# Layer 0 of a hybrid diffusion backbone: a shorter projection prologue, and the work between attention tiles pinned to a place

## The chip, the cores and the metric

The kernel runs on one core of one Trainium2 chip, in one launch. The core has five engines with instruction streams of their own: TensorE (PE, matmul), VectorE (DVE), ScalarE (ACT), GpSimd (POOL) and SyncE (SP, which here only issues DMAs). The metric is device time in microseconds (us); the kernel is timed in several runs and one more execution is profiled.

## The reference

Two layers run over 1024 latent tokens and a context prefix of 256 tokens, width 1024, all in float32. The change touches layer 0 alone. Its core, cut:

```
h_lat = rms_norm(x_lat, norm_g) * (1 + sc) + sh           # adaLN from c; h_ctx alike from c_ctx
aq, ak, av, ag, bq, bk, bv, bg = split_cols(h @ w_in, (512, 128, 128, 512, 512, 128, 128, 512))
aq, ak = rms_norm(aq, q_gain), rms_norm(ak, k_gain)       # A alone
aq, ak, bq, bk = rope(...)                                # latent tokens alone
oa = softmax(aq ka^T / 8) va                              # A: 8 heads, 2 key heads, keys = ctx + all latents
ob = softmax([bq kb^T / 8 + band, sink]) vb               # B: ctx + latents within 128, sink logit per head
y = concat([oa * silu(ag), ob * silu(bg)]) @ w_out        # also for the context tokens
x = x + g * y
```

Layer 1 (a conformer convolution and a 2-D neighbourhood attention) and a final RMSNorm follow.

## The kernel before, in words

**Precision.** Each float32 matmul is done as three matmuls of a fast format: every operand is split into a high part (a cast on ACT) and a low part (a subtraction on POOL or DVE, `split`, lines 307 to 310), and `mm3` (lines 327 to 329) adds high x high, high x low and low x high.

**Units.** Layer 0's attention is cut into four units `u`, each of four query heads that share one key head. Units 0 and 1 are A (global, with the RMSNorm of queries and keys), 2 and 3 are B (banded, with a sink). They run in the order `ORDER = (2, 3, 0, 1)`: B, B, A, A. I call them first to fourth unit, and the last one the fourth.

**Projection.** `proj_qkv(u)` computes queries, keys and values of a unit in ten blocks of 128 tokens (`j` = 0, 1 context, 2 to 9 latent), 24 matmuls of 384 columns each (PSUM name `pq`), two blocks to a step `jp`. A block is copied to SBUF (`pc`), normed (units 0 and 1: square, reduce, a reciprocal root by Newton steps, ten small multiplications, line 835), rotated (`rt`, lines 846 to 850), and then taken by `qk_tail`: three PE transposes (`trk`), splits, a store of the queries to DRAM (`Q<-qs`) and keys into the SBUF tile `KA`. `proj_gate(u, ms)` computes the SiLU gate of a unit in six pieces (`m` = two halves of the channels, `c` = three chunks of 256, 512 and 512 tokens; 24 matmuls, name `pg`) and stores it to DRAM (`G<-sg`). Both are generators that yield three times a block, which I call pieces: a piece is some 8 matmuls.

**Attention.** `attn_gen` runs over groups (a unit and a block of 128 queries, in the order `QORD`, ten to a unit), and in a group over tiles of 128 keys: two score matmuls (`st`), for a band edge a mask, exponent on ACT, `split` into `ph` and `pl`, and three more matmuls (`ov`) three tiles later (`LOOK0`). B has 42 tiles a unit, A 84. Each tile yields twice: a step. Before a group's tiles stands its preparation (`attn_prep`): it loads the queries (`QH`, `QL`), takes a bound of the scores by extra matmuls with a maximum on DVE (`mx`, `mp`), and writes it with the sink into `QL`; it is spread over the tiles of the group two ahead. A group ends with `finish`: transposes of the denominators, products (`y`), the gate (`gt`, loaded by `gate()` at the middle tile) and a store (`Od<-y`), or, in the last unit, a split in place. `KB`, a copy of the keys in another tile, is made by `load_kb` in two DMAs at a unit's first group; there is one `KB` for all units, and two `KA` and two `V`.

**What lies where.** `weave(main, n, fill, k)` takes `n` attention steps and lays `k` pieces of `fill` between them. The fill's instructions get a lower priority (`later(80)`); the compiler's list scheduler orders each engine's stream by priority and readiness as it estimates them. With `lag` > 0, each fill instruction is also held behind the score matmul `lag` scores back (`issue_after(sts[-lag])`, on PE's stream alone). Before the change layer 0 never uses it, so that fill may stand in PE's stream far ahead of its place in the program. The attention steps of layer 0 are 12 of preparation, then 84, 84, 168 and 168, and fill is laid as follows: the whole first projection and half of its gate run alone (`solo`), the other half in the first 9 steps; then the next unit's projection and half of its gate in the middle of a unit's steps, the other half of its gate at the start of the next unit; the last `NLAST` steps of a unit (28 or 48) have none. In the fourth unit lie the loads of earlier outputs (`load_oh`) and the output projection (`po`) of the first two units in 65 steps, of the third in 41, of the fourth (`final_proj`, with the residual's norm and the next layer's h, `norm_h`) in the rest, for the chunks that are complete; the last chunk comes after the attention.

**Modulation.** The pieces of the projections also tick `mods`, which computes the rest of the adaLN vectors (`pm`, from weights `mw`): every `TICK0` = 1 piece while solo, every `TICK1` = 3 afterwards.

## Time and profile before

| what | us |
|---|---|
| median of 3 runs | 1579.01 (1578.08 to 1581.34) |
| the profiled execution | 1581.59 |
| its span, first to last instruction | 1579.8 |
| PE busy in the span | 1469.3 |
| DVE, POOL, ACT busy | 1086.9, 794.1, 748.8 |

A row of the profile names the source line, the engine, the operation, out<-in by the program's tile names, and the shapes; "x" is a count. Stretches are in us from the span's start. "PEld" is the load of a matmul's stationary operand, which overlaps the matmuls. The granted clock is a share of TensorE's full clock. Layer 0 covers about the first 950 us.

### The profile page before, as it was taken

The page shows a single profiled execution, that of the slowest core. Times are in us where ns is not written, and L with a number is a line of the kernel's source. Part 1 is how long each engine was busy: PE and PEld are TensorE (multiplying, and loading weights), DVE is VectorE, ACT ScalarE, POOL GpSimd, SP SyncE. Part 2 cuts the span into 40 slices and gives each one's busy share as a digit, 9 for nine tenths or more (in the row PEclk, how much of TensorE's full clock was granted, in tenths as well). Part 3 has the DMA queues.
Part 4 walks back from the last instruction along what each step waited for, and adds up shares of the span by engine and source line. Part 5 has one row for each costly group of instructions (what it writes and reads, how often), then busy time and mean ns, then how long its engine had stood idle before and what let it go on. Part 6 is the DMA issues. An engine that isn't in the chain of part 4 may idle for free.

```text
span 1579.8 us, 21684 instructions
## 1 busy us (share of the span) xinstructions
PE 1469.3 (93%) x7084; PEld 1172.7 (74%) x7084; DVE 1086.9 (69%) x2279; ACT 748.8 (47%) x1418; POOL 794.1 (50%) x637
## 2 busy tenths in 40 slices
PE   6899999998998999999999879999989999989995
PEld 2785987886886767876766657888877878768874
DVE  2833576588589865566677856999738466787866
ACT  3722333443435555447556654433334355554563
POOL 3531352553445666557556754664532244364665
PEclk8899999998999999999999989999999999979997
DMA  9473324422312253222112022222595577967632
GB/s 367 151 238 127 114 84 153 137 76 90 110 44 82 87 195 129 64 57 62 41 30 88 7 66 77 86 68 72 175 271 194 186 215 218 284 191 231 187 110 107
DMA packets 158105, 208.23 MB, mean 132 GB/s; under 512 B 15068, under 2 KB 96168, under 8 KB 157992
## 3 DMA queue, kind: packets, MB, share of 16 engines
q1 hardware_dynamic: 151328, 195.27, 39.1%
q10 hardware_dynamic: 6664, 11.57, 2.2%
q8 instruction: 56, 0.92, 0.3%
q14 instruction: 57, 0.47, 0.1%
HBM read 152.27 MB, written 53.22 MB: 130 GB/s over the span
## 4 chain that ended last, share of the span: by engine, by line
PE 73%; DVE 15%; DMA 6%; ACT 2%; issue 2%; POOL 1%; SPq 0%; ACTq 0%; DVEq 0%; POOLq 0%
PE p L327 6%; PE p L328 6%; PE p L329 6%; PE ov L447 4%; PE ov L449 4%; PE po L327 4%; PE po L329 4%; PE po L328 4%; PE ov L448 4%; PE st L491 4%; PE st L495 4%; PE pq L327 3%; PE pq L328 3%; PE pq L329 3%; PE pg L329 2%
## 5 line engine op out<-in xcount | busy, mean ns | idle before, releaser
L310 POOL TENSOR_TENSOR pl<-pf,ph 128x512 fp32r<-128x512 f32 (+4 forms) x321 | 392.9, 1235 | 362.8 <-ACT ph L307 280.0
L503 ACT ACTIVATE pf<-st 128x512 f32<-128x512 f32 x284 | 166.0, 596 | 213.7 <-PE st L495 159.2
L310 POOL TENSOR_TENSOR wl<-wr,wh 128x512 fp32r<-128x512 f32 (+2 forms) x131 | 168.7, 1300 | 187.8 <-ACT wh L307 145.9
L307 ACT CAST ph<-pf 128x512 fp32r<-128x512 f32 (+4 forms) x364 | 210.0, 588 | 19.6 <-PE ov L448 9.5
L327 PE MATMUL p<-hh,wh 128*128 128x512 f32 x448 | 180.0, 402 | 11.7 <-ACT wh L307 6.2
L328 PE MATMUL p<-hl,wh 128*128 128x512 f32 x448 | 179.6, 402 | 1.2 <-POOL hl L310 1.2
L329 PE MATMUL p<-hh,wl 128*128 128x512 f32 x448 | 176.3, 399 | 0.0
L491 PE MATMUL st<-QH,KAt 128*128 128x512 f32 (+4 forms) x364 | 142.5, 392 | 7.6 <-DVE pf L500 4.7
L447 PE MATMUL ov<-ph,Vt 128*128 128x512 f32 (+4 forms) x364 | 141.9, 390 | 5.5 <-DVE y L652 3.4
L449 PE MATMUL ov<-pl,Vt 128*128 128x512 f32 (+4 forms) x364 | 142.5, 391 | 4.5 <-POOL pl L310 3.5
L448 PE MATMUL ov<-ph,Vt 128*64 128x512 f32 (+4 forms) x364 | 139.9, 384 | 0.0
L495 PE MATMUL st<-QL,KBt 68*128 68x512 f32 (+4 forms) x364 | 135.8, 386 | 0.0
L307 ACT CAST wh<-wr 128x512 fp32r<-128x512 f32 (+2 forms) x134 | 80.8, 612 | 98.4 <-PE p L328 21.2
L1068 DVE SCALAR_TENSOR_TENSOR cps<-U,taps,cps 128x512 f32<-128x512 f32 x184 | 126.3, 749 | 0.9
L327 PEld LDWEIGHTS p<-hh,wh 128*128 128x128 f32 x448 | 85.4, 191 | 33.0 <-ACT wh L307 7.1
L615 DVE TENSOR_REDUCE mp<-mx 128x1 f32<-128x512 f32 x128 | 85.7, 682 | 25.7 <-PE mx L614 25.2
L328 PEld LDWEIGHTS p<-hl,wh 128*128 128x128 f32 x448 | 85.5, 191 | 21.7 <-POOL hl L310 2.2
L329 PEld LDWEIGHTS p<-hh,wl 128*128 128x128 f32 x448 | 85.3, 190 | 20.6 <-issue 0.5
L449 PEld LDWEIGHTS ov<-pl,Vt 128*128 128x128 f32 x364 | 70.5, 194 | 28.9 <-POOL pl L310 9.9
L327 PE MATMUL pq<-wh,hh 128*128 128x384 f32 x256 | 88.5, 346 | 2.8 <-ACT hh L307 2.8
L491 PEld LDWEIGHTS st<-QH,KAt 128*128 128x128 f32 x364 | 70.0, 192 | 26.3 <-ACT pf L503 6.9
L329 PE MATMUL pq<-wh,hl 128*128 128x384 f32 x256 | 87.4, 341 | 0.0
(277 smaller groups left out, 3482.6 us busy)
## 6 DMA issues: line engine op xcount, KB each, us to landing
mw<-in_mod_w_dram SPq DMA_DIRECT2D x16, 1024.0 KB, 5.7
Q<-qs SPq DMA_DIRECT2D x40, 256.0 KB, 2.1
QH<-Q SPq DMA_DIRECT2D x80, 128.0 KB, 2.7
mw<-in_mod_w_dram SPq DMA_DIRECT2D x16, 512.0 KB, 6.5
wr<-in_od_d_dram SPq DMA_DIRECT2D x32, 256.0 KB, 2.9
wr<-in_ev_qkv_dram SPq DMA_DIRECT2D x16, 384.0 KB, 5.1
KAt<-KD SPq DMA_DIRECT2D x16, 384.0 KB, 5.8
wr<-in_od_wo_dram SPq DMA_DIRECT2D x22, 256.0 KB, 3.3
```

The lines of the kernel that those rows point to most:

```text
L307: acts.append(SC.copy(hi, src))
L310: (GP if leng == "g" else VE).tensor_tensor(lo, src, hi.bitcast(F32), op=ALU.subtract)
L327: PE.matmul(o, lh, rh, start=first, stop=False)
L328: PE.matmul(o, lh, rl, start=False, stop=False)
L329: PE.matmul(o, ll, rh, start=False, stop=last)
L447: PE.matmul(o, V[:, 64:192], ph[:, :n], start=(t == 0), stop=False)
L448: PE.matmul(g.ov[0:64, q0 : q0 + n], V[:, 0:64], ph[:, :n], start=False, stop=False)
L449: PE.matmul(o, V[:, 64:192], pl[:, :n], start=False, stop=(last and g.sink is None))
L491: sts.append(PE.matmul(st[:, :n], KA[:, cs], g.QH[:, q0 : q0 + n], start=True, stop=False))
L495: PE.matmul(st[:, :n], KB[0:68, cs], g.QL[0:68, q0 : q0 + n], start=False, stop=True)
L503: acts.append(SC.activation(pf[:, :n], st[:, :n], AF.Exp, scale=1.0 if g.bias else SCALE))
L1068: VE.scalar_tensor_tensor(pc, uc, w, pc, op0=ALU.mult, op1=ALU.add)
```

## The change

The constants `N0`, `NLAST`, `GB` and `NFILL` go; `LAG0 = 3` comes, `TICK1` goes from 3 to 2, `O1` from (6, 65, 41, 14) to (6, 80, 42, 22). `proj_qkv` takes a list of block pairs, so that a unit's projection can be cut in two, and ends by emptying its `tails`. `load_g0`, which brought the first unit's gate weights through the attention's `ph` and `pl` buffers, goes; those weights now use the projection's weight buffers like the others. Solo are now only the first six blocks of the first unit. Then one list says what is laid into the attention steps, with every fill pinned three scores back: the first unit's other four blocks into the 12 preparation steps, its gate for chunk 1 into 6, the rest of its gate and the second projection into 70, the second gate and the third projection into 72, the third gate, fourth projection and fourth gate into 200. The key copies are cut at 384 and 768; the banded units copy the last part only at their third group. In layer 0 `gate()` is called at a group's last tile. The output projection is pinned likewise, and has 80 and 42 steps instead of 65 and 41; the final part then has 28 steps for 22 pieces instead of 44 for 14. `ready` and the assertions on it only check the order while the program is built, and leave no instruction.

```
-            if t == len(g.tiles) // 2:
+            if t == (len(g.tiles) // 2 if layer[0] else len(g.tiles) - 1):
                 g.gate()
...
-        for ks in (slice(0, 512), slice(512, NTOK)):
+        i = QORD.index(qb)
+        parts = {0: ((0, 384), (384, 768), (768, NTOK))} if u < 2 else {0: ((0, 384), (384, 768)), 2: ((768, NTOK),)}
+        for k0, k1 in parts.get(i, ()):
+            ks = slice(k0, k1)
             SY.dma_start(KBs[u][0:64, ks].bitcast(F32), KAs[u][0:64, ks].bitcast(F32))
...
-                gw[u] = load_g0(u) if u == ORDER[0] else load_w0("ev_g", u)
+                gw[u] = load_w0("ev_g", u)
...
-        def proj_qkv(u, w):
-            wh, wl = w or load_w0("ev_qkv", u)
-            new_kv(u)
-            for jp in range(5):
+        def proj_qkv(u, jps, w=None):
+            if jps[0] == 0:
+                gw[u, 0] = w or load_w0("ev_qkv", u)
+                new_kv(u)
+            wh, wl = gw[u, 0]
+            for jp in jps:
...
+            while tails:
+                qk_tail(*tails.pop(0))
...
-        for _ in fill0(0, w0):
+        def gates(u, *cs):
+            return proj_gate(u, [(m, c) for c in cs for m in range(2)])
+
+        for _ in proj_qkv(ORDER[0], (0, 1, 2), w0):
             pass
...
-        for k in range(4):
-            u = ORDER[k]
-            n = NSTEP[u // 2] + (12 if k == 0 else 0)
-            if k < 3:
-                n0 = N0[1 + u // 2] if k else N0[0]
-                n1 = n - n0 - NLAST[u // 2]
-                weave(main, n0, proj_gate(u, gblocks(k)[1]), 9, False)
-                weave(main, n1, fill0(k + 1), NFILL[k], False)
-                weave(main, NLAST[u // 2], iter(()), 0, False)
-            else:
-                weave(main, GL, proj_gate(u, gblocks(k)[1]), 18 - 3 * GB, False)
+        A, B, C, D = ORDER
+        full = range(5)
+        for n, fill, k in ((12, [proj_qkv(A, (3, 4))], 12),
+                           (6, [gates(A, 1)], 6),
+                           (70, [gates(A, 0, 2), proj_qkv(B, full)], 42),
+                           (72, [gates(B, 1, 0, 2), proj_qkv(C, full)], 48),
+                           (188 + GL, [gates(C, 1, 0, 2), proj_qkv(D, full), gates(D, 1, 0, 2)], 66)):
+            weave(main, n, chain(*fill), k, False, True, LAG0)
...
-        weave(main, O1[1], out0_part(parts[0]), 48, False)
-        weave(main, O1[2], chain(load_oh(parts[1]), out0_part(parts[1])), 30, False)
+        weave(main, O1[1], out0_part(parts[0]), 48, False, True, LAG0)
+        weave(main, O1[2], chain(load_oh(parts[1]), out0_part(parts[1])), 30, False, True, LAG0)
```

More of the change, by code (lines that the diff above doesn't have):

```diff
@@ L66 @@
 LATE = 100
-GB = 2
-NFILL = (39, 39, 36)
 GL = 12
 HV = 'gggvvvvg'
-O1 = (6, 65, 41, 14)
-TICK0, TICK1 = (1, 3)
+O1 = (6, 80, 42, 22)
+LAG0 = 3
+TICK0, TICK1 = (1, 2)
 PLAN = 'p0mmnbwmm1h2nbhnbh'
@@ L570, in kv_tiles, with load_kb @@
             KV.append((KA, KB, V))
-    def load_kb(u):
-        for ks in (slice(0, 512), slice(512, NTOK)):
+    def load_kb(u, qb):
+        i = QORD.index(qb)
+        parts = {0: ((0, 384), (384, 768), (768, NTOK))} if u < 2 else {0: ((0, 384), (384, 768)), 2: ((768, NTOK),)}
+        for k0, k1 in parts.get(i, ()):
+            ks = slice(k0, k1)
+            assert all((u, j) in ready for j in range(ks.start // P, ks.stop // P))
             SY.dma_start(KBs[u][0:64, ks].bitcast(F32), KAs[u][0:64, ks].bitcast(F32))
@@ L591, in gate @@
         def gate():
+            assert all((u, m, 0 if qb < 2 else (1 if qb < 6 else 2)) in ready for m in range(2))
             gt = a0.tile([P, 2, P], F32, tag="gt", name=nm("gt"), bufs=2)
@@ L611, in maxes @@
                 if not isb:
+                    assert all((u, j) in ready for j in range(10))
                     for k in range(2):
@@ L620, in maxes @@
                     mo = (lo - (qb - 1)) * P
+                    assert all((u, j) in ready for j in range(lo, hi))
                     mx = bank("mx", nm("mx"))
@@ L663, in group0 @@
         hs = (u - 2) * 4
[L664 removed]
+        g = Group(load_q=load_q, start=lambda: load_kb(u, qb), bias=False, ahead=lambda t: None, gate=gate, v=lambda k: V0s[u][:, k, :], load_v=None, maxes=maxes, nmp=1 if qb < 2 else (2 if isb else 3),
                   sink=(sink[:, hs : hs + 4], sink8[:, hs : hs + 4]) if isb else None, skm=lambda: sk, k=lambda: (KAs[u], KBs[u]),
```

27 lines of the change are left out of this document (4 added, 23 removed).

## The prediction

> **What bounds the kernel now.** I read the page first (busy shares), then the span cut into stretches, then the same cut for single tiles, then the waits. The page:
>
> ```profile
> span 1579.8 us, 21684 instructions
> PE 1469.3 (93%) x7084; PEld 1172.7 (74%) x7084; DVE 1086.9 (69%) x2279; ACT 748.8 (47%) x1418; POOL 794.1 (50%) x637
> ```
>
> TensorE carries the kernel, but 93% busy does not say that only 7% can be had: the ends of matmuls are modelled. I count matmuls per stretch instead. The stretches of layer 0 that hold its attention (columns: stretch, length, then busy us and count for PE, PEld, DVE, ACT, POOL, granted clock, DMA):
>
> ```profile
> 220.00:280.00 60.00, 57.22 (x303) 47.53 (x296) 43.09 (x99) 25.98 (x58) 26.81 (x20) 0.97 0.41 137
> 280.00:340.00 60.00, 60.00 (x332) 52.91 (x331) 41.48 (x129) 25.52 (x55) 29.30 (x22) 1.00 0.36 115
> 340.00:400.00 60.00, 51.71 (x250) 39.84 (x249) 49.97 (x119) 24.82 (x54) 29.80 (x23) 0.91 0.25 82
> 400.00:460.00 60.00, 60.00 (x319) 52.91 (x317) 42.29 (x107) 26.70 (x53) 29.07 (x20) 1.00 0.27 84
> 460.00:520.00 60.00, 55.10 (x273) 43.11 (x273) 55.38 (x150) 25.63 (x56) 30.22 (x24) 1.00 0.26 79
> 520.00:580.00 60.00, 57.54 (x268) 44.23 (x266) 41.81 (x80) 33.80 (x65) 38.93 (x28) 1.00 0.32 105
> 580.00:640.00 60.00, 56.30 (x268) 44.40 (x268) 33.75 (x59) 28.95 (x49) 36.93 (x28) 1.00 0.47 161
> 640.00:700.00 60.00, 60.00 (x293) 48.79 (x292) 35.93 (x66) 28.95 (x50) 34.50 (x26) 1.00 0.23 67
> 700.00:760.00 60.00, 57.54 (x242) 41.12 (x240) 42.52 (x79) 41.99 (x71) 42.51 (x33) 0.97 0.19 54
> 760.00:800.00 40.00, 40.00 (x194) 32.24 (x193) 26.16 (x49) 21.30 (x38) 23.22 (x18) 1.00 0.11 31
> 800.00:840.00 40.00, 34.76 (x142) 25.00 (x141) 32.74 (x64) 23.23 (x41) 20.84 (x16) 0.91 0.13 37
> 840.00:880.00 40.00, 37.84 (x175) 29.12 (x174) 32.14 (x55) 24.80 (x45) 27.24 (x21) 1.00 0.24 83
> 880.00:950.00 70.00, 56.33 (x218) 40.52 (x218) 48.16 (x87) 44.17 (x86) 43.79 (x37) 0.85 0.15 50
> ```
>
> Two stretches are full: 400 to 460 gives 188 ns a matmul (projections of 384 columns laid into attention), 640 to 700 gives 205 ns (output projection into attention). At 188 ns the stretch 340 to 400 needed 47.0 us and lost 13.0; 460 to 520 lost 8.7. At 205 ns, 520 to 580 and 580 to 640 lost 5.1 each, 700 to 760 lost 10.4, 760 to 800 0.2, 800 to 840 10.9, 840 to 880 4.1, 880 to 950 25.3. With 3.0 in 220 to 280 that is 86 us: all that any reordering of this part can win.
>
> Why there: the fill (work laid between attention tiles) has no lower bound on its place, and is used up early. The output projection shows it:
>
> ```profile
> 580.00:640.00 60.00, 29.93 (x135) 23.20 (x136) 7.01 (x11) 1.00 0.47 161
> 640.00:700.00 60.00, 36.69 (x166) 28.05 (x165) 9.95 (x16) 1.00 0.23 67
> 700.00:760.00 60.00, 4.87 (x23) 3.97 (x23) 1.99 (x3) 0.97 0.19 54
> 760.00:800.00 40.00, 20.53 (x93) 15.62 (x91) 10.37 (x16) 1.00 0.11 31
> 800.00:840.00 40.00, 3.80 (x18) 2.93 (x18) 2.19 (x4) 0.91 0.13 37
> ```
>
> These are po's rows alone. In the program they belong to the last unit's attention, yet that unit's keys are copied only at about 735 us (the last of the eight rows below), and 300 of the 576 po matmuls ran before. Where po is thin (700 to 760, 800 to 840) PE is not full: attention alone does not fill it.
>
> ```profile
> L575 SPq DMA_DIRECT2D KBt<-KAt x8: 498/512/567, 99.5 to 734.6; - x8
> ```
>
> **The change, part by part.** The matmuls, splits and weights are the same; only order, waits and a few DMAs change.
>
> Prices used below: the split of a weight piece on POOL and ACT and a maximum on DVE (the page's groups), store and load of queries (DMA issues, us to landing), and a stretch of projection blocks alone:
>
> ```profile
> L310 POOL TENSOR_TENSOR wl<-wr,wh 128x512 fp32r<-128x512 f32 (+2 forms) x131 | 168.7, 1300 | 187.8 <-ACT wh L307 145.9
> ...
> L307 ACT CAST wh<-wr 128x512 fp32r<-128x512 f32 (+2 forms) x134 | 80.8, 612 | 98.4 <-PE p L328 21.2
> ...
> L615 DVE TENSOR_REDUCE mp<-mx 128x1 f32<-128x512 f32 x128 | 85.7, 682 | 25.7 <-PE mx L614 25.2
> ```
> ```profile
> Q<-qs SPq DMA_DIRECT2D x40, 256.0 KB, 2.1
> QH<-Q SPq DMA_DIRECT2D x80, 128.0 KB, 2.7
> ```
> ```profile
> 91.30:95.40 4.10, 4.10 (x24) 4.10 (x25) 1.11 (x2) 0.59 (x1) 1.57 (x1) 1.00 0.86 265
> ```
>
> *Start.* Attention begins behind six blocks of the first unit instead of ten and three gate blocks. Before, the solo stretch also carried eight modulation steps; some went in pairs between gate matmuls:
>
> ```profile
> 120.41 0.97 PE pm L179 x2
> ...
> 130.56 0.98 PE pm L179 x2
> ...
> 153.46 1.84 PE pm L179 x12
> ```
>
> Eight pairs at 0.98 us are 7.8 us; sixteen in a row take about 1.9 (the chain's third row: twelve of them in 1.84). 6 us lost by placement, and with half as many ticks left in the solo stretch I let that go. Against it: the first unit's gate weights no longer come through the attention's idle buffers but through the projection's, so they wait for its last matmuls. Cast and subtraction of a piece are 0.6 and 1.3 us (the first two rows), four pieces in a row: 0 (covered by the first scores) to 6 us; I take 2, since the two raw pieces are loaded ahead. The first chain (query load, maxima, exponent, scores) is covered by the four remaining blocks and two gate blocks, 96 x 0.17 (24 block matmuls in 4.10 us) + 48 x 0.21 = 27 us. Net -4, range -6 to +6.
>
> *Projections in order of need.* The third unit's projection (with its norm chain on VectorE) lies in the second unit's attention, both before and after: 30 pieces in 45 steps, 22.5 tiles. The same mix stood at 280 to 400:
>
> ```profile
> 280.00:400.00 120.00, 20.37 (x63) 11.64 (x63) 0.00 (x0) 15.04 (x27) 0.96 0.30 99
> ```
>
> This row is st's alone. 27 tiles (ACT's count of st), and VectorE busy 41.48 + 49.97 = 91 us. For 22.5 tiles that is 76 (all of it by tiles) to 91 (none); I take 83, which at the highest share seen, 55.38 of 60, stands for 90 us. PE wants 240 x 0.171 = 41 for the blocks, 7 x 0.205 = 1.44 a tile (five matmuls, its share of masks and maxima), 32, and some 7 for transposes and modulation: 80. So 10 us are lost to VectorE if it never waits, 19 if the 91 holds; I take 15, nearer the upper end as its chain has latencies. Before, this pocket and the fourth unit's, 340 to 520, lost 21.7. The fourth unit's norm chain now spreads over some 90 steps of the third unit's attention. Net -6, range -12 to +4.
>
> *Handover to the third unit.* Its projection ends at step 160, its first maxima (all ten key blocks) come from step 164, its first score at step 180. Before, it ended 20 steps earlier, and more by hoisting. Twenty steps at about 1.2 us are 24 us for the last block's norm chain, the transposes, store and load of the queries (2.1 and 2.7 us) and the maxima on VectorE, ten of 0.68 at most. Nearly enough; pinned fill covers only three tiles. +8, range 0 to +14.
>
> *Gates and fourth unit behind.* 520 to 640 lost 10.2 where output-projection loads and the handover fell together. Loads now come in the last unit. -6, range -10 to 0.
>
> *Output projection over 80 and 42 steps, pinned.* The pockets 700 to 880 (25.6 us) fill up: po for 61 tiles, like 640 to 700, which is full with 166 po matmuls in it. What stays is a few us at the seams. -20, range -24 to -8.
>
> *Tail.* 22 pieces in the last 28 steps, where 14 stood in 44. The norm and h steps of two chunks crowd VectorE while the 14 last tiles run; before, that stretch (880 to 950) lost 25.3 with DVE at 48.16 of 70. I leave it at 0, range -8 to +12: the last chunk's chain stays alone either way.
>
> *Small edits.* Four more key-copy DMAs at about 0.5 us of SP's queue each: nothing, SP is no bound; behind them stand query loads used a group later. The third piece of a banded unit waits for key blocks six to nine, and only behind that queue. The gate load at a group's last tile instead of its middle:
>
> ```profile
> DMA to landing us min/median/max: 2.4/2.5/6.5
> ```
>
> Three tiles of look-ahead, over 6 us, hide 2.5; without them it would be 2.5 us a group at VectorE. The lag adds a wait on PE's queue order alone.
>
> Sum: -4 - 6 + 8 - 6 - 20 + 0 = -28. The profiled execution took 1581.59 us (span 1579.8); 1553.6 by it. The median of the runs, 1579.01, is 2.6 lower: 1551.
>
> **The clock as a weight on this.** After a hole the granted clock is halved:
>
> ```profile
> 376.00:381.00 5.00, 3.26 (x14) 1.68 (x12) 4.97 (x12) 2.07 (x5) 3.53 (x3) 1.00 0.18 52
> 381.00:391.00 10.00, 7.67 (x21) 5.73 (x22) 8.75 (x21) 3.81 (x10) 4.08 (x4) 0.51 0.23 81
> ```
>
> This loss is inside the 86 us, so my terms hold it. [...]
>
> **The rivals.**
> *Slower: the pin starves PE.* Fill may not pass the score three tiles back, so a wait of attention can be covered only by what three tiles carry: six steps with 0.33 to 0.67 pieces of some 1.4 us, 3 to 6 us; and where a stage is bound by VectorE, none is left. Place: the 40 group starts, where maxima, exponent and QL follow one another. For it: these steps are a row of short VectorE instructions, and DVE had 92% in 460 to 520.
>
> ```profile
> PE mx L614 <- DVE mp L615: 4.3, 12, 0.7
> ```
>
> Against: PE's waits there are at most 0.7 us, though with free fill beside them. It decides from 28 / 40 = 0.7 us uncovered a group; at 1.0 the time is 1579 + 12 = 1591.
> *Handed back: the holes only move.* The pockets of the last unit fill, but the third unit's attention, which had 300 po matmuls, and VectorE in the second unit give most of it back, or the compiled order moves little. Bad ends of handover, projections and tail (+14, +4, +12) against the -20, -6 and -4 of the other terms sum to 0: 1579.
> *All pockets close.* Good ends of start, projections, gates and output projection (-6 - 12 - 10 - 24), handover 0: 1527; a tail at -8 gives 1519. For it: 400 to 460 and 640 to 700 run full at VectorE shares of 70 and 60%.
>
> **How the numbers follow.** My sum (1535 to 1570): 0.54. All pockets close (1519 to 1535): 0.12. Handed back (1570 to 1582): 0.14. Starved (over 1582): 0.20. A measurement here tells about 0.2%, 3.2 us, from no change: faster 0.54 + 0.12 + 0.07 = 0.73, within 0.07, slower 0.20. The range 1528 to 1586 leaves out half of the good case and most of the starved one, about 0.2. The likeliest case's own range is 1535 to 1570.
>
> **What would show it.** Right: first scores near 100 us; po spread evenly through the last unit, none before its keys are copied; 700 to 880 at the count of 640 to 700; the chain without runs of DVE in the last unit. The projection step: DVE over 90% in the second unit. The handover: PE idle before the third unit's first score. Wrong: PE's counts falling in every stretch alike, with idle time released by DVE at group starts (starved), or a last unit that is full and a second unit or tail that grew by as much (handed back).

## The result: slower by 0.9%, and the profile after

The changed kernel takes 1593.76 us (median of 4 runs, 1592.32 to 1595.91) where the kernel before takes 1580.04 beside it: a ratio of 1.0093, 95% interval 1.0079 to 1.0106. The forecast was 1551, with 1528 to 1586 as its range. The rival "the pin starves PE", priced at 1591, is the nearest of the four cases.

The page after, first its head:

```profile
span 1591.8 us, 21662 instructions
PE 1463.9 (92%) x7084; PEld 1173.5 (74%) x7084; DVE 1082.6 (68%) x2279; ACT 748.3 (47%) x1418; POOL 797.8 (50%) x637
```

The busy sums of the engines are the same within 6 us, so the 12 us by which the span grew come from where the work stands, not from more work. The span before, cut at the first score of the first, second, third and fourth unit, at the last score, and at the first product of layer 1 (columns as in the prediction's first table of stretches: stretch, length, then busy us and count of PE, PEld, DVE, ACT, POOL, granted clock, DMA):

```profile
132.70:328.80 196.10, 192.48 (x1042) 164.58 (x1041) 124.56 (x327) 76.90 (x167) 75.76 (x59) 0.99 0.36 117
328.80:500.50 171.70, 159.34 (x797) 130.27 (x796) 138.19 (x364) 71.21 (x150) 84.52 (x64) 0.97 0.24 78
500.50:734.90 234.40, 226.00 (x1066) 177.08 (x1065) 155.48 (x295) 125.66 (x226) 145.21 (x110) 0.99 0.31 101
734.90:926.50 191.60, 174.22 (x764) 130.88 (x763) 144.76 (x263) 120.94 (x219) 120.31 (x97) 0.95 0.13 42
926.50:949.00 22.50, 17.77 (x61) 12.89 (x61) 10.97 (x18) 9.34 (x17) 11.37 (x9) 0.85 0.42 135
```

The same cut after the change:

```profile
102.90:284.20 181.30, 172.52 (x896) 139.78 (x896) 109.20 (x294) 76.01 (x162) 78.67 (x61) 0.99 0.41 129
284.20:456.60 172.40, 157.91 (x802) 126.78 (x801) 134.29 (x349) 74.06 (x153) 80.83 (x62) 0.96 0.32 104
456.60:695.30 238.70, 219.19 (x1030) 176.02 (x1030) 166.59 (x333) 125.29 (x233) 143.63 (x106) 0.96 0.21 67
695.30:928.40 233.10, 222.37 (x1027) 176.09 (x1026) 135.21 (x250) 118.21 (x204) 129.00 (x98) 0.97 0.25 78
928.40:972.80 44.40, 28.06 (x128) 22.06 (x126) 33.30 (x56) 22.23 (x47) 22.65 (x21) 0.86 0.27 91
```

Attention begins 29.8 us earlier (102.9 against 132.7), and layer 1 begins 23.8 later (972.8 against 949.0). The first unit's row shows a part of how: 202 ns a matmul (181.30 over 896) against 188 before. The third unit's goes from 220 to 232, and only the fourth, which now holds the output projection, gets denser (251 to 227). The last row, from the last score to layer 1, doubles.

Matmul kinds differ between these rows, so I use one measure below. Each recorded matmul is charged its time in a dense run, and the rest of the stretch is called its loss. The charge is 172 ns for 384 columns (after the change, those of pq start 0.17 us apart from 87.01 to 88.57 us) and 231 for 512, and for the small ones what their own dense runs give; that for 512 is from the products of layer 1, rows of p alone:

```profile
1046.00:1116.00 70.00, 70.00 (x302) 56.10 (x301) 5.51 (x8) 4.78 (x8) 1.00 0.19 62
```

As "end of layer 0" I take the 300th product of layer 1, since part of layer 0's tail still lies between the first ones; what follows is work that no edit but one touches. The medians are of all runs; ends, rests and losses are of the one profiled execution of each kernel, which lay within 3 us of its median (f2 4.8 below, k1 3.3 above), so a difference of a few us between two kernels rests on single executions. The kernels from e1 on are told below. All kernels in this measure (us; losses in the stretch from 60 us to the first score, in units 1 and 2, in 3 and 4, and from the last score to the end of layer 0):

| kernel | median | end of layer 0 | rest | before attention | units 1+2 | units 3+4 | end |
|---|---|---|---|---|---|---|---|
| before | 1580.04 | 1027.9 | 551.9 | 13.7 | 38.7 | 53.4 | 15.8 |
| the change | 1593.76 | 1046.0 | 545.8 | 7.5 | 50.4 | 57.0 | 26.4 |
| e1 no pins | 1566.22 | 1009.3 | 555.6 | 7.8 | 29.4 | 53.9 | 13.6 |
| e2 output pinned only | 1571.39 | 1024.5 | 545.1 | 8.4 | 27.7 | 56.4 | 26.3 |
| e3 units pinned only | 1597.76 | 1039.7 | 555.9 | 7.9 | 51.9 | 55.5 | 18.6 |
| e4 old output steps | 1585.41 | 1037.6 | 546.0 | 8.2 | 51.1 | 53.6 | 18.8 |
| f1 units 12 back | 1579.38 | 1031.4 | 547.1 | 8.3 | 42.5 | 56.7 | 18.0 |
| k2 units 40 back | 1573.22 | 1026.5 | 545.6 | 7.3 | 32.6 | 66.5 | 15.4 |
| f2 kernel before, pinned | 1619.23 | 1056.1 | 556.5 | 12.3 | 63.9 | 56.1 | 17.6 |
| g1 change, no norm | 1578.78 | 1030.5 | 544.8 | 7.8 | 44.3 | 46.0 | 27.3 |
| g2 no pins, no norm | 1545.88 | 998.1 | 543.7 | 8.6 | 22.6 | 47.5 | 13.7 |
| h1 pinned, dense | 1588.25 | 1038.2 | 546.9 | 7.7 | 49.8 | 61.2 | 14.1 |
| h2 no pins, dense | 1566.96 | 1009.4 | 554.2 | 8.1 | 28.7 | 53.3 | 13.9 |
| k1 free inside its entry | 1591.08 | 1035.7 | 556.9 | 7.9 | 54.4 | 53.8 | 15.0 |
| h3 no pins, old prologue | 1586.29 | 1032.6 | 554.1 | 11.1 | 41.6 | 59.9 | 14.5 |
| k3 no pins, four blocks | 1584.70 | 1034.3 | 549.3 | 8.7 | 49.6 | 56.7 | 14.2 |
| i1 no pins, late masks | 1563.38 | 1008.7 | 553.4 | 8.2 | 26.8 | 55.0 | 13.0 |
| m1 later bound | 1586.45 | 1038.8 | 545.7 | 8.3 | 51.0 | 50.3 | 23.4 |
| m2 output pinned, old steps | 1565.44 | 1019.8 | 544.9 | 7.8 | 28.8 | 59.0 | 18.6 |
| m3 as m2, 12 back | 1566.56 | 1021.2 | 546.4 | 8.0 | 29.3 | 60.9 | 17.2 |

In the changed kernel the losses grow by 11.7 in units 1 and 2, 3.6 in 3 and 4 and 10.6 at the end, and shrink by 6.2 before attention. That is 19.7, where layer 0 ends 18.1 later. Layer 1 then takes 6.1 less.

The output projection did move as the diff says (rows of po alone, third unit, fourth unit, end):

```profile
456.60:695.30 238.70, 0.00 (x0) 0.00 (x0) 0.00 (x0) 0.96 0.21 67
695.30:928.40 233.10, 112.86 (x486) 85.66 (x486) 37.39 (x56) 0.97 0.25 78
928.40:972.80 44.40, 20.95 (x90) 15.56 (x90) 9.58 (x16) 0.86 0.27 91
```

The end before held 48 of them:

```profile
926.50:949.00 22.50, 13.97 (x48) 10.99 (x48) 5.14 (x7) 0.85 0.42 135
```

TensorE stands more often in each of the first three units. Its largest waits after the change (what PE was to run, what it waited for: us in total, times, longest), first two rows from the first unit, three from the second:

```profile
PE st L488 <- ACT pf L500: 4.0, 2, 3.5
PE mx L606 <- DVE QL L423: 3.3, 4, 1.7
PE trk L855 <- DVE KAt L307: 4.7, 1, 4.7
PE mx L606 <- DVE QL L423: 4.6, 5, 1.7
PE trk L855 <- DVE modT L185: 2.6, 1, 2.6
```

trk is a transpose of the fill itself (new queries and keys), so the fill too stands in PE's order. The third unit got projections and gates for the output projection, and they do not fill it. Its waits after the change, and then the same for the third unit before:

```profile
PE trn L422 <- DVE nmt L412: 11.4, 4, 7.0
PE mx L619 <- DVE mp L620: 2.3, 2, 1.3
PE st L488 <- ACT pf L500: 1.9, 5, 0.5
PE mx L606 <- DVE QL L423: 1.3, 4, 0.5
PE ov L444 <- DVE y L658: 1.0, 1, 1.0
```
```profile
PE mx L614 <- DVE mp L615: 2.3, 7, 0.4
PE trn L425 <- DVE nmt L415: 0.7, 1, 0.7
```

All waits that the profile lists for these units add up to 8.3, 14.5 and 19.3 us after the change, and to 3.7, 11.9 and 8.2 before.

trn is the transpose of a group's bound, the last but one step of its preparation (QL is written from it). Its longest wait in the order of time, first PE's stream (start, length, and in brackets the idle time before and what ended it):

```profile
603.17 0.34 PE L326 MATMUL pq<-wh,hl 128*128 128x384 f32 x1
603.53 0.50 PE L619 MATMUL mx<-KAt,QH 128*128 128x512 f32 x1
611.01 0.37 PE L422 MATMUL trn<-ident,nmt 128*4 128x128 f32 x1 [6.98 <-DVE nmt L412]
```

and VectorE's in the same stretch:

```profile
603.39 1.84 DVE L829 SCALAR_TENSOR_TENSOR pc<-pc,nr,gain 128x64 f32<-128x64 f32 x9
605.26 0.92 DVE L454 STREAM_TRANSPOSE r<-ov 64x256 f32<-64x256 f32 x2
606.21 0.69 DVE L620 TENSOR_REDUCE mp<-mx 128x1 f32<-128x512 f32 x1
...
607.29 0.68 DVE L620 TENSOR_REDUCE mp<-mx 128x1 f32<-128x512 f32 x1
...
609.60 1.35 DVE L412 TENSOR_SCALAR nmt<-m 128x4 fp32r<-128x4 f32 x1
```

VectorE works through a key's norm, a finished group's transposes and two maxima before it gives nmt; TensorE stands 7 us, because its next instruction in the written order is the transpose. The instruction that gives nmt lasted 1.35 us here, where the middle one of its 56 takes 171 ns; why is not shown. The hole and what follows, by stretches:

```profile
603.90:611.00 7.10, 0.13 (x1) 0.00 (x0) 7.02 (x21) 0.13 (x1) 1.53 (x1) 0.86 0.00 0
611.00:621.00 10.00, 9.74 (x39) 7.82 (x40) 8.05 (x18) 4.64 (x10) 3.63 (x3) 0.76 0.16 52
```

VectorE is busy for 7.02 of the 7.10 us, and the granted clock is 0.76 in the ten us after. The clock's records of the kernel before and of the changed one hold only full and half; here it is half over this stretch, of which TensorE stood idle for the first 2 us:

```profile
609.00:615.82 6.82, 4.81 (x13) 3.60 (x14) 5.39 (x11) 0.12 (x1) 1.53 (x1) 0.50 0.13 38
```

Added up from 60 us to the end of layer 0, the clock is at half for 51.6 us before, 68.3 after the change and 44.4 without pins (e1 below). At half, matmuls of 512 columns start 0.43 us apart (612.41 to 614.12), at full 0.23 (621.15 to 621.84). So half of the difference is about the most that this can have cost: 8.4 us of the 19.7, and 12 of what the pins cost. The end of layer 0 has its own waits:

```profile
PE trs L251 <- DVE acc L952: 5.2, 1, 5.2
PE po L324 <- ACT hh L304: 4.3, 1, 4.3
```

### The profile page after: what moved, and what is told of

The parts are those of the page before. It is cut to its first block, busy times and chain, and to the rows that moved or that the text cites. A ratio compares the mean times of both kernels' runs of the same rounds, so it can differ in the third digit from the quotient of the medians.

```text
span 1591.8 us, 21662 instructions
## 1 busy us (share of the span) xinstructions
PE 1463.9 (92%) x7084; PEld 1173.5 (74%) x7084; DVE 1082.6 (68%) x2279; ACT 748.3 (47%) x1418; POOL 797.8 (50%) x637
## 4 chain that ended last, share of the span: by engine, by line
PE 68%; DVE 17%; DMA 6%; issue 3%; POOL 3%; ACT 3%; SPq 0%; DVEq 0%; ACTq 0%; POOLq 0%
PE p L326 6%; PE p L324 6%; PE p L325 6%; PE st L488 4%; PE ov L444 4%; PE ov L446 4%; PE ov L445 4%; PE po L324 4%; PE st L492 4%; PE po L325 4%; PE po L326 3%; PE pq L326 2%; PE pq L325 2%; PE pg L324 2%; PE pq L324 2%
## 5 line engine op out<-in xcount | busy, mean ns | idle before, releaser
L307 POOL TENSOR_TENSOR wl<-wr,wh 128x512 fp32r<-128x512 f32 (+2 forms) x135 | 173.1, 1293 | 145.8 <-ACT wh L304 115.5
L304 ACT CAST ph<-pf 128x512 fp32r<-128x512 f32 (+4 forms) x364 | 210.4, 588 | 13.3 <-PE ov L445 2.2
L488 PE MATMUL st<-QH,KAt 128*128 128x512 f32 (+4 forms) x364 | 143.2, 393 | 13.9 <-ACT pf L500 9.1
L620 DVE TENSOR_REDUCE mp<-mx 128x1 f32<-128x512 f32 x128 | 86.0, 684 | 64.6 <-PE mx L619 63.9
L488 PEld LDWEIGHTS st<-QH,KAt 128*128 128x128 f32 x364 | 69.6, 191 | 38.0 <-ACT pf L500 17.1
L325 PE MATMUL pq<-wl,hh 128*128 128x384 f32 x256 | 87.1, 340 | 0.0
```

Of the source, the lines that this page charges most:

```text
L304: acts.append(SC.copy(hi, src))
L307: (GP if leng == "g" else VE).tensor_tensor(lo, src, hi.bitcast(F32), op=ALU.subtract)
L325: PE.matmul(o, lh, rl, start=False, stop=False)
L488: sts.append(PE.matmul(st[:, :n], KA[:, cs], g.QH[:, q0 : q0 + n], start=True, stop=False))
```

## The experiments

The first theory was the rival's: the pin takes from TensorE the fill that it would have run ahead, and it stands where attention waits. Against it stood three others: that TensorE stands behind the norm chain of VectorE, which now lies among more steps; that the list itself (density and order of the fill) is at fault and the pin harmless; and that the shorter prologue or the new output steps cost the time. "Lag" is how many scores back an instruction of the fill is held.

**The two pins apart (e1, e2, e3).** e1 takes the lag from both; e2 from the units alone; e3 from the output projection alone.

```
-            weave(main, n, chain(*fill), k, False, True, LAG0)
+            weave(main, n, chain(*fill), k, False)                      # e1, e2
...
-        weave(main, O1[1], out0_part(parts[0]), 48, False, True, LAG0)
-        weave(main, O1[2], chain(load_oh(parts[1]), out0_part(parts[1])), 30, False, True, LAG0)
+        weave(main, O1[1], out0_part(parts[0]), 48, False)              # e1, e3
+        weave(main, O1[2], chain(load_oh(parts[1]), out0_part(parts[1])), 30, False)
```

> The changed kernel (1593.8 us) with no pin at all in layer 0; everything else of the change stays. Theory P (the pin starves PE in the units' stages: the three first units lose 86 us of PE's full pace after, 58 before): fill runs ahead again, some 25 us come back in the units, but the output projection is again used up early; 1570 to 1580. Theory T (the tail: 44 us from the last score to the first matmul of layer 1, 22 before): with free output projection the final part starts earlier and 10 to 20 us come back in the tail; 1575 to 1583, the units unchanged. Theory O (the order of need itself: late projections with their norm chains are what costs): no gain, 1590 to 1600.

> The changed kernel with the pin taken off the units' fill (projections, gates) and left on the output projection. Theory P: the three first units return to about 60 us of loss, the fourth keeps its 21; 1565 to 1575. Theory T: nothing in the tail changes; 1590 to 1595. Theory O: 1590 to 1598.

> The changed kernel with the pin left on the units' fill and taken off the output projection. Theory T: the final part is free to run early, the tail falls from 44 us toward 25; 1575 to 1582. Theory P: the units still lose 86 us, little changes; 1588 to 1595.

Measured: e1 1566.22 (ratio to the kernel before 0.9909, 0.989 to 0.9928), e2 1571.39 (0.9943, 0.9921 to 0.9965), e3 1597.76 (1.0106, 1.009 to 1.0123). At the end of layer 0 the pin on the units costs 30.4 us (e3 less e1) or 21.5 (the change less e2); in the median 31.5 or 22.4. The pin on the output projection costs 15.2 or 6.3 at that point. (That e3 is the slowest of the four by the median comes from layer 1, 555.9 us against 545.8.) e1 came out below the range of theory P, e3 above it; and of theory T this much holds, that the end falls from 26.4 to 18.6 when the output projection is free. Without pins the change beats the kernel before. e1's units by stretches:

```profile
103.20:287.80 184.60, 182.70 (x990) 150.56 (x989) 118.70 (x299) 78.50 (x170) 79.33 (x63) 1.00 0.45 145
287.80:483.50 195.70, 187.51 (x986) 159.43 (x984) 150.47 (x405) 79.84 (x168) 94.22 (x70) 0.99 0.27 88
483.50:716.90 233.40, 226.17 (x1063) 179.07 (x1064) 153.29 (x293) 125.39 (x225) 143.96 (x110) 0.98 0.32 101
716.90:909.90 193.00, 173.56 (x764) 130.06 (x763) 144.29 (x263) 121.37 (x219) 120.18 (x97) 0.96 0.13 41
```

Free fill packs 1976 matmuls into the first two units, at 192 ns each (380.3 us); pinned, the same units held 1698 at 208 ns (353.7 us). The 278 that were held back went into the later units, and there they cost full time. Losses in units 3 and 4 are 53.9 without pins and 57.0 with both. The waits that the profile lists for the first three units fall from 42.1 us with both pins to 17.1 (1.8, 8.2 and 7.1); the largest that are left in the third:

```profile
PE mx L619 <- DVE mp L620: 3.2, 4, 1.7
PE trn L422 <- DVE nmt L412: 2.2, 2, 2.0
```

In e2's third unit and fourth unit, one sees why the output projection's pin brings nothing:

```profile
484.00:687.60 203.60, 181.67 (x770) 129.69 (x771) 141.00 (x276) 120.28 (x216) 132.85 (x102) 0.97 0.33 105
687.60:907.20 219.60, 212.62 (x1008) 168.27 (x1007) 133.56 (x244) 114.13 (x198) 120.02 (x93) 1.00 0.15 46
```

The fourth unit is full (218 ns a matmul), and the third is now the empty one (264 ns). Losses of 44.6 and 11.8 stand for 18.3 and 35.6 without the pin. The hole changed its place.

**The old steps of the output projection (e4).**

```
-O1 = (6, 80, 42, 22)
+O1 = (6, 65, 41, 14)
```

> The changed kernel with the output projection's old share of the steps (65, 41, and 44 left for the final part, 14 of its pieces in them), pins as in the change. Theory T: the final part begins 16 attention steps earlier and its norm chains lie beside attention; tail 44 to about 30, 1578 to 1586. Theory P: 1590 to 1596, since the units are untouched.

Measured: 1585.41 (1.0048, 1.0029 to 1.0067). Layer 0 ends 8.4 us earlier than with the change, 7.6 of it at the end (26.4 to 18.8). So the new counts cost about 8, most of it in the tail.

**A longer lag, and the pin on the old order (f1, f2).**

```
-            weave(main, n, chain(*fill), k, False, True, LAG0)
+            weave(main, n, chain(*fill), k, False, True, 12)             # f1, output projection free
...
-                weave(main, n1, fill0(k + 1), NFILL[k], False)
+                weave(main, n1, fill0(k + 1), NFILL[k], False, True, 3)   # f2, on the kernel before; its gate weaves alike
```

> The changed kernel with the units' fill pinned 12 tiles back instead of 3, the output projection free. With 3 tiles and the output projection free it took 1597.8 us, with no pin 1566.2. Theory R (what matters is how far fill may run ahead: with 12 tiles, some 30 us, PE has fill for waits of 7 us): 1568 to 1582. Rival S (the pin costs whatever its length, since it spreads the fill evenly and the third unit is then thin): 1590 to 1598.

> The kernel before with its units' fill pinned three tiles back and nothing else changed. If the pin itself is the loss, it costs here too: 1590 to 1610, with the losses in the units up by 20 or more (its stretches without fill are then really without). If the loss needs the new order (late projections right ahead of the unit that uses them), the kernel before stays within 1575 to 1585.

Measured: f1 1579.38 (0.9996, 0.9986 to 1.0007), f2 1619.23 (1.024, 1.0217 to 1.0263). Twelve scores back takes 8.3 us off e3's layer 0 (most of the rest of the 18 in the median is layer 1); on the old list the pin costs 28.2 there, about what it costs on the new, and f2 came out above its range. So the new list is not what makes the pin dear. The loss lies in f2's first two units again, 63.9 against 38.7.

**Is it the norm chain? (g1, g2)** RMSNorm of queries and keys is left out in the units that have it, with the pins (g1) and without (g2).

```
-                if u < 2:
+                if False:
```

> The changed kernel, pins as they are, without the RMSNorm of queries and keys in the two A units (square, reduction, Newton steps and multiplications are left out, some 8 us of VectorE a block pair, ten pairs). Theory V (PE stands at transposes of the bound or of new keys because VectorE is behind with the norm chain, and pinned fill can't step in): much of the pin's 27 us goes; 1560 to 1575. Rival S (thin fill, whatever VectorE does): gains only as much as the kernel without pins does, 5 to 10 us; 1583 to 1590.

> The changed kernel without pins and without the same RMSNorm of queries and keys; the partner of the run before. Theory V: little is gained over 1566.2, since free fill covers these waits already: 1558 to 1565, and the distance between the two is under 12 us instead of 27. Rival S: the distance stays 20 or more.

Measured: g1 1578.78, g2 1545.88, so the pins cost 32.9 with no norm in the kernel, where they cost 27.5 with it (the change less e1). Both kernels gain by the missing work, and neither time lies in a range named for it, but the distance, which was to decide, stays; so do the waits listed for the first three units, 29.3 us with pins and 8.2 without. The norm chain as the reason fell. It is a part of what VectorE does in the longest hole.

**Is it the density of the list? (h1, h2)** The same fill in fewer steps, so that each of three tiles carries more: 118 steps for the last entry of the list instead of 200, and the output projection over 100 and 62. The final part's 22 pieces then have 70 steps instead of 28.

```
-GL = 12
+GL = -70
...
-O1 = (6, 80, 42, 22)
+O1 = (6, 100, 62, 22)
```

> The changed kernel with its pins (three tiles back, units and output projection), but the fill set denser and earlier: the last entry's 66 pieces in 118 steps instead of 200, and the output projection begins 70 steps before the fourth unit and has 100 and 62 steps. That is about the spread that the compiler makes by itself where nothing is pinned. Theory D (the loss is how the fill is rationed: a unit holds about 36 us of holes until its fill passes some 210 us of matmuls, so evenly thin fill is worst): layer 0 ends near where it does without pins, 1570 to 1580. Theory R (the loss is that fill can't step in locally when a group's preparation waits for VectorE): pins stay, so 1585 to 1595.

> The same denser setting without pins. Where fill runs ahead by itself anyway, the setting should change little against the kernel without pins (1566.2): both theories 1560 to 1572.

Measured: h1 1588.25 (1.0058, 1.0043 to 1.0073), h2 1566.96 (0.9923, 0.9904 to 0.9942). This setting gives back 7.8 of layer 0: 12.3 in the tail (26.4 to 14.1), where the final part has its longer room, of which units 3 and 4 take 4.2 again; the first two lose as before (49.8). Density as the main reason fell. h2 is e1 within 1 us: where fill is free, the steps that the list gives it hardly matter.

**Is room inside an entry enough, and how far must fill run ahead? (k1, k2)** k1 holds the fill only behind the last score ahead of its own entry of the list; k2 has a lag of 40. In both the output projection is free.

```
+        first = len(sts)
...
-                    if lag and len(sts) >= lag:
+                    if lag and not layer[0] and first:
+                        cx.enter_context(tc.issue_after(sts[first - 1].ins))
+                    elif lag and layer[0] and len(sts) >= lag:              # k1
...
-            weave(main, n, chain(*fill), k, False, True, LAG0)
+            weave(main, n, chain(*fill), k, False, True, 40)                # k2
```

> The changed kernel with the output projection free and the units' fill pinned only to the last score ahead of its entry in the list (after 18, 88 and 160 steps), so that it may go anywhere inside its entry but not ahead of it. Pinned three tiles back in the same place it took 1597.8 us, without pins 1566.2. Theory R (fill has to be free to step in where attention happens to wait): most of the 30 us come back though each unit still gets about the same work, 1568 to 1580. Theory D (what a unit is given in all decides): 1588 to 1598.

> The changed kernel with the output projection free and the units' fill pinned 40 tiles back, near a whole banded unit. 3 back took 1597.8, 12 back 1579.4 (of which some 9 us lie in layer 1, whose order happens to differ), none 1566.2. Theory R: 40 tiles are as good as none, 1562 to 1572. Theory D: the fill still can't leave its unit by much, 1574 to 1582.

Measured: k1 1591.08 (1.0064, 1.004 to 1.0088), k2 1573.22 (0.9953, 0.9936 to 0.9969). With the output projection free, layer 0 ends at 1039.7, 1031.4, 1026.5 and 1009.3 for lags of 3, 12, 40 and none, and the losses of the first two units go 51.9, 42.5, 32.6, 29.4. Each further reach pays. Room that ends at an entry's edge does not: k1's first two units lose 54.4, though it may reach far back within an entry. So, as far as these runs show, it is the run ahead from one entry's stretch into the one before that the pin takes away. (k1 lies in the range of theory D, k2 between the two ranges.)

**Is standing at the preparation the cause, or where it shows? (m1)** With both pins, the transpose of the bound comes seven steps after VectorE's part instead of three, in layer 0.

```
-        for _ in range(3):
+        for _ in range(3 if layer[0] else 7):
             yield
         tr2 = bank("mx", nm("trn"))
```

> The change with both pins; in the first layer alone the norms' reduction on VectorE gets seven stretches of fill instead of three before TensorE is given the transpose that turns them. If the pin costs because TensorE stands in its order at the steps that each unit's group preparation waits for (the transpose waited 7.0 us once behind the norms), the first layer ends 5 to 15 us before 1046.0 and the run takes 1579 to 1589; if this standing is only where a general shortage of fill becomes visible, the wait moves to the next step, the first layer ends within 4 us of 1046, and the run takes 1590 to 1597.

Measured: 1586.45 (1.0067, 1.0044 to 1.0089). Layer 0 ends 7.2 us earlier. Waits of the third unit:

```profile
PE trn L422 <- DVE nmt L412: 5.2, 3, 2.5
PE mx L606 <- DVE QL L423: 4.8, 3, 2.6
PE ov L444 <- DVE y L658: 4.0, 3, 1.8
```

The wait at the transpose halves (11.4 to 5.2), and those for QL and y grow (1.3 to 4.8, 1.0 to 4.0). All waits listed in the third unit add up to 18.9 us, where they were 19.3: they moved. Of the 36.7 us that both pins cost in layer 0 a later place for this one step returns 7, nearly all of it in units 3 and 4 (57.0 to 50.3), and the first two units' losses stay (50.4, 51.0). By its time and its layer 0, m1 came out in the range of the first theory; by its waits it does what the second said. I read it so: standing at this step is a part of the cause, and the larger part is the shortage of fill, which then shows at the next step.

**The prologue without pins (h3, k3).** h3 is e1 with ten blocks and half of the gate ahead of attention, k3 with four blocks; the first entries of the list, not shown, take what is left (in h3 the other half of the gate in 9 steps and the second projection in 79, in k3 six blocks in the 12 preparation steps).

```
-        for _ in proj_qkv(ORDER[0], (0, 1, 2), w0):
+        for _ in chain(proj_qkv(ORDER[0], tuple(range(5)), w0), proj_gate(ORDER[0], [(0, c) for c in range(3)])):   # h3
+        for _ in proj_qkv(ORDER[0], (0, 1), w0):                                                                       # k3
```

> The changed kernel without pins and with the prologue of before (all ten blocks of the first unit and half of its gate alone, the other half in the first 9 steps). If the short prologue is what makes the kernel without pins faster than before, this one loses most of the 14 us: 1574 to 1582. If the order behind it does (gates and projections laid without gaps), it stays at 1564 to 1570.

> The changed kernel without pins, its attention begun behind four projection blocks instead of six. With ten blocks and half a gate it took 1586.3, with six 1566.2. If the short prologue pays because more work is left to lie under attention, two blocks more are worth some 3 to 8 us: 1558 to 1564. If six already cover the first chain and PE's first blocks wait for h anyway, 1564 to 1572.

Measured: h3 1586.29 (1.0045, 1.003 to 1.006), k3 1584.70 (1.0027, 1.0013 to 1.0041), e1 1566.22. The shorter prologue is worth 20 us without pins, but a still shorter one loses 18. Only 3.3 of h3's 23.3 in layer 0 lie before attention; 12.2 lie in the first two units and 6.0 in the others. So the length of the prologue works less by itself than by how full the units behind it come out in the compiled order. Both times lie outside every range named for them, and why four blocks lose is open. h3 has the prologue of before, the rest of the change and no pin, and it is 0.45% slower than the kernel before: of the prologues tried, the new order gains only with six blocks.

**Layer 1 (i1).** Layer 1 is not touched, yet the rest behind layer 0 is 543.7 to 549.3 us in twelve of the twenty kernels and 551.9 to 556.9 in the other eight. i1 is e1 with the first loads of layer 1's masks issued behind a store, as the kernels with the shorter rest have them.

```
+                        vst = SY.dma_start(VD[i][:, bl[k][0] : bl[k][0] + e - k], sv[:, k:e].bitcast(F32))
+                        vst0.extend([vst] * (i == 0))
...
+                with tc.issue_after(vst0[-2].ins) if gi == 0 else ExitStack():
+                    SY.dma_start(bms[b], a["d_bm"][hd, hf, :, BMO[b] : BMO[b] + n])
```

> The changed kernel without pins, with the first loads of layer 1's bias masks issued behind a store of that layer's values instead of ahead of it. From the 300th matmul of layer 1 to the end the kernels take either about 545 us (the change, and three of its variants) or about 555 (without pins; before: 552), and in the slow ones these loads stand ahead of stores and weights on SP's queue. If that order is the cause: 1566.2 less 7 to 10, 1556 to 1559. If it only goes along with it: 1564 to 1568.

Measured: 1563.38 (0.9898, 0.9883 to 0.9913), the best of those with the whole computation, but only 2.2 us of rest less than e1 (553.4). That order of loads explains little. Most of the difference lies in the stretch from 90 to 200 us after the end of layer 0, rows of p alone, in the changed kernel:

```profile
1136.00:1246.00 110.00, 98.22 (x436) 74.94 (x435) 9.69 (x24) 11.52 (x27) 1.00 0.71 223
```

and in e1:

```profile
1099.30:1209.30 110.00, 93.35 (x399) 70.40 (x398) 8.38 (x21) 10.11 (x23) 0.97 0.64 201
```

399 products against 436. This count parts all twenty kernels: 395 to 419 products in the eight with the longer rest, 433 to 440 in the twelve others. The DMA engines do not: they are less busy in e1 (0.64 against 0.71), but not in the kernel before, which has a long rest too:

```profile
1117.90:1227.90 110.00, 96.49 (x416) 74.76 (x415) 9.19 (x23) 10.87 (x25) 0.95 0.72 217
```

What comes late is open.

**A best version (m2, m3).** Free units, the output projection pinned 3 or 12 back, old step counts.

```
-O1 = (6, 80, 42, 22)
+O1 = (6, 65, 41, 14)
...
-            weave(main, n, chain(*fill), k, False, True, LAG0)
+            weave(main, n, chain(*fill), k, False)
...
-        weave(main, O1[1], out0_part(parts[0]), 48, False, True, LAG0)
+        weave(main, O1[1], out0_part(parts[0]), 48, False, True, 12)      # m3 alone; the other weave alike
```

> The units' fill free, the output projection pinned three tiles back, and its step counts as they were before (6, 65, 41, 14 for 6, 80, 42, 22). If the stretch behind the last score is set by the step counts whatever the fill, this takes 8 us off the kernel with only the output projection pinned (1571.4): 1561 to 1566. If the step counts cost only where the units are pinned too, 1569 to 1574.

> As the kernel beside it (units' fill free, old step counts), with the output projection pinned twelve tiles back instead of three. If the length of the lag sets what the pin on the output projection costs (15.2 us of the first layer at three, none without), the first layer ends by 1012 to 1018 and the run takes 1555 to 1565; if any pin on it costs the same, it is within 3 us of the kernel beside it.

Measured: m2 1565.44 (0.9916, 0.9886 to 0.9946), m3 1566.56 (0.9929, 0.9905 to 0.9952). The old counts take 7.7 off e2's end (26.3 to 18.6) whether or not the units are pinned. The lag of 12 brings nothing: of m3's two expectations the second held, that any pin on the output projection costs the same. With little other fill left, the third unit is empty whatever the lag (46.5 and 46.7 lost). In time e1, i1 and m2 can't be told apart: m2's layer 0 ends 10.5 us later than e1's and its layer 1 is 10.7 shorter.

## Why the prediction was wrong, step by step

| term | predicted, range | the change | without pins (e1) |
|---|---|---|---|
| start | -4, -6 to +6 | -6.2 | -5.9 |
| first unit | not priced | +9.6 | -2.1 |
| projections in the second unit | -6, -12 to +4 | +2.1 | -7.2 |
| handover and gates, third unit | +8 - 6 | +16.9 | -0.9 |
| output projection in the fourth | -20, -24 to -8 | -13.3 | +1.4 |
| tail | 0, -8 to +12 | +10.6 | -2.2 |
| sum | -28 | +19.7 | -16.9 |

(Differences of the loss to the kernel before. Layer 0's end moved by +18.1 and -18.6.)

*The step that failed is "The lag adds a wait on PE's queue order alone".* It was put among the small edits and priced at nothing. It cost 36.7 us of layer 0 with the output projection's part (the change less e1), 21.5 to 30.4 for the units alone. Six pairs of kernels, the units pinned three scores back in one and free in the other, show it at the end of layer 0 (in some the output projection's pin goes with it): 36.7, 30.4, 21.5, 28.2 on the old list, 32.4 without the norm, 28.8 in the dense setting. What came in place of nothing are waits of TensorE in its own order: 42.1 us listed in the first three units against 17.1 without pins. But for the handover's +8, the terms beside it were sized as if fill could still run ahead. The start, second unit and third unit without pins are near the forecast's values or better (-5.9, -7.2, -0.9); with ten or four blocks ahead of attention they would not be (h3, k3). The pins are not the whole of the miss: without them the kernel is 0.9%, some 14 us, faster than before, half of the 28 forecast.

*The rival named the right mechanism and half of the place.* Its sign was "PE's counts falling in every stretch alike, with idle time released by DVE at group starts". They fell in the first three units and not in the fourth (227 ns a matmul against 251), and the idle time, most of it ended by DVE, is what the rows of the first three show. But the group starts, where it put the whole price, carry a part: m1 moves one such step and gets 7 back, and in the second unit the fill's own transposes wait too (trk, 7.3 us). That its 1591 lies near the 1593.76 is in part luck: its 40 us at 40 starts are near the 36.7, but the tail's +10.6 and layer 1's -6.1 are not in it.

"Against: PE's waits there are at most 0.7 us, though with free fill beside them" took one row for all. The same view of the kernel before, from 60 to 960 us, has longer ones at preparations (mx, trn) and at new keys (trk):

```profile
PE mx L622 <- DVE mp L623: 3.7, 1, 3.7
PE trk L858 <- DVE KAt L310: 3.7, 1, 3.7
PE trn L425 <- DVE nmt L421: 3.7, 3, 2.8
```

And the row that it took did not move: in the third unit that wait of mx for mp is 2.3 us in all, before and after. What grew there is the wait at trn, 0.7 to 11.4.

*"All that any reordering of this part can win" was read off pockets that can't be closed one at a time.* The output projection's term held in its place (-13.3 in the fourth unit, 227 ns a matmul). Yet it came out of the third unit. Over all twenty kernels, units 3 and 4 together lose 46 to 67 us, and 50 to 67 with the norm in; the kernel before has 53.4. No order that was tried moved this sum below 50.3. The first two units moved more, 22.6 to 63.9. With the six-block prologue they follow how far fill may run ahead; h3 and k3, without pins, lose 41.6 and 49.6 there, so the prologue counts too. The prediction had the warning in a rival, "Handed back", by which the third unit's attention gives back what the fourth gains, and in its price for that rival put the bad end of the handover for it.

*The tail at 0 was mis-sized.* It measured +10.6, inside its range, and e4 gives 7.6 of it to the new step counts: 22 pieces in 28 steps, where 14 stood in 44, put 90 po matmuls behind the last score instead of 48.

*The clock.* The hole ahead of the ten slow us in the prediction's two rows is the wait of trk for KAt, 3.7 us from 379.58, which the cut at 381 divides. Nor is the clock halved after every hole: the wait of mx for mp shown above, 3.7 us from 352.02, left it at 1.00 over the next 10.25 us. So these rows do not show what kind of hole halves it. The terms held the loss of before, and the time at half grew from 51.6 us to 68.3; the records allow at most 8.4 us for that.

*Layer 1* was taken as fixed. It moved by -6.1, and in other kernels by -8.2 to +5, so a gain in layer 0 is read at the end of layer 0 first.

## What to carry to other kernels

A lower bound on where filler may stand is not a free tidiness: on an engine that stands at the next instruction of its order, as TensorE did here (6.98 us at one transpose), it forbids the early work that covers later waits, so price it by the waits that would be bare without that work, not by the waits seen with it. And since the prologue alone moved this kernel by 20 us, try such a bound on more than one order before it is called the cause. Before a pocket of idle time is counted as gain, name where the work that fills it now stands and what that place loses. When an untouched stage follows, cut the span where the touched one ends and read both parts.

## What the hardware showed that was not expected

- The same work of layer 1 takes 543.7 to 549.3 us or 551.9 to 556.9 by the compiled order, with most of the difference in one stretch, where TensorE starts 395 to 419 products or 433 to 440. Why is open.
- A hole of 7.1 us on TensorE left a granted clock of 0.76 over the ten us behind it, so it cost more than its length. The clock fell to half 5 us after the hole began and was there from 609.00 to 615.82, 4.8 us of it behind the hole, where matmuls of 512 columns start 0.43 us apart instead of 0.23. Two holes of 3.7 us in the kernel before differ: behind the one from 379.58 the clock is 0.50 up to 391.22, behind the one from 352.02 it is 1.00 up to 366.
- Prologue length is not monotone: ten, six and four blocks without pins take 1586.29, 1566.22 and 1584.70 us.
